# Fewer gathers in the gate phase, fewer U steps beside the drain, and the first splits of v one step earlier

## The chip, the cores and the metric

One core of one Trainium2 chip runs the whole program. The metric is device time in microseconds: the kernel before takes 1535.39 us (median of 3 runs, 1534.54 to 1535.76). The profiled execution, from which every duration below is read, took 1524.62 us, of which 1522.8 us lie between its first and its last instruction.

## The reference, cut to what matters

A decoder layer on 512 tokens of width 1024, in float32: a token mixer (gated linear attention beside a state-space group), and then PEER, a retrieval of single-neuron experts. The change lies in PEER alone:

```
q = (xt @ w_query)                      # 8 heads x 2 halves, 128 keys each
s = einsum('thpd,hpkd->thpk', q, sub_keys)
top_s, top_i = top_k(s, 16)             # per half; then the best 16 of the 16x16 sums
gate = softmax(best_s)
act = einsum('td,ted->te', x_blk, u[i_blk])
hid = gelu(act) * g_blk
out = einsum('te,ted->td', hid, v[i_blk])
```

There are 16384 experts (128 x 128 keys), u and v hold a row of 1024 for each, and each token uses 128 of them.

## The kernel before, in words

**Two ways to the experts.** The first 384 tokens (TD) don't gather. For them the kernel computes the activations of all 16384 experts, in 128 steps of 128 experts: U step e computes u·x for its 128 experts and 384 tokens, 24 matmuls in 8 parts of 3 (`u_part`, `rhs_part`, L857), because float32 is kept by splitting each operand into a high and a low part (`split`, L103 and L104: ScalarE copies the high part `uh`, L91, and VectorE, or GpSimd in some stages, subtracts to get the low part `ul`). V step e adds hid·v for the same 128 experts, 18 matmuls (6 groups of 3). The last 128 tokens gather their rows of u and v by an indirect DMA (`gather`, L1134), 128 gathers of u and 128 of v of 512 KB each; VectorE uses each in one instruction of 128x1024 (`use`, L100). Two gathers stay pending, so the use of one is written when the second after it is issued. There are three buffers (`gat`).

**The stages.** (1) The mixers. (2) The queries and scores, with 6 U steps in between. (3) The route: VectorE works out which experts each token has (`select`, four times two halves, `spread`), while TensorE is given 17 U steps, so that 23 are done. ScalarE's pieces of `ties(t)` (tile `k`), which wait for an earlier `select` to give up the buffer, are written between parts of the U steps. The low parts are made on GpSimd here. (4) The gate phase: 48 units of 8 tokens. For each unit VectorE builds one-hot tiles (A, eq, B), TensorE multiplies them (`pg`, L1185, 16 matmuls), ScalarE copies the gates of the later experts into `stage`, and VectorE multiplies the gates into `ring` for the U steps that are done. Between the units stand 32 U steps (steps 23 to 54), whose low parts VectorE makes, and 12 gathers, one after every fourth unit. Every 8 units the stage tile (128 partitions x 69 x 64, in two buffers) is written to device memory (`gd`), on ScalarE's DMA queue, in pieces of 256 bytes. (5) The drain: after the last unit the last stage tile is written out while U steps 55 to 58 run. (6) The V loop: V step e beside U step e+59 (as long as there is one), with the remaining gathers spread over it; `gload` reads the gates of step e+59 back from `gd` into the ring (59 steps long). The kernel's own constants are RING = 59 and LEFT, the number of U steps beside the drain.

**What sets the order.** Each engine runs its instructions in the order in which the program writes them. All loads of u, v, `gd` and the weights are issued by one queue (SyncE's, "SPq" in the profile), in order too: a load that has to wait holds all loads behind it. A U step's rows of u are loaded two steps ahead, and split one step ahead. Gathers are issued by GpSimd.

**Memory at the border of stages 4 and 6.** The gate phase's pool `gp` (A, eq, B, two stage tiles) is closed after the last unit, and the pool `vp` of the V loop (high and low parts `vh`, `vl` of v, raw blocks `vr`, the split gates `hh`, `hl`) takes the same place. `reuse_waits="tile"` makes each new tile wait only for the old tiles whose bytes it takes. In both pools the names lie one after the other in the order in which they are first asked for, each with all its buffers. In `gp` that is A (2 x 2048 bytes of a partition), eq (2048), B (2 x 4096) and stage (2 x 17664). In the kernel before the order in `vp` is vh (3 x 2048), vl (3 x 2048), vr (4 x 4096), hh (2 x 1536), hl (2 x 1536). Of the buffers of one name the first request takes the lowest, the second the highest, the next ones follow downwards.

Of the kernel before, what the change touches and what calls it, by code (L numbers as in the profile page):

```python
# [8 lines left out]
F32R = mybir.dt.float32r  # L9
# [16 lines left out]
TD = GT * 128  # L26
# [37 lines left out]
class Layer:  # L64
# [791 lines left out]
    def experts(self):  # L856
# [103 lines left out]
        def ties(t):  # L960
            x = (kp if t % 2 else self.kr).tile([128, 2, 8, 16, 16], F16, name="k8", tag="k8", bufs=1)
            for e in range(2):
                for g in (slice(0, 4), slice(4, 8)):
                    pieces.append((t, x[:, e, g], bc(tif[:, t, g, e, :], 3, 16)))
            TIE[t] = x
# [8 lines left out]
        def select(t):  # L974

            while any(p[0] == t for p in pieces):
                piece()
            ii = kp.tile([128, 2, 8, 16], F32, name="ii", bufs=2)
            for e in range(2):
                oh = c.tile([128, 8, 16, 16], F16, name="gat", tag="gat", bufs=3)  # L980
                tt(oh, bc(CF[0][:, e, t], 2, 16), bc(itj if e else its, 1, 8), OP.is_equal if e else OP.is_ge)
                tt(oh, oh, TIE[t][:, e], OP.mult)
                for n in (8, 4, 2):
                    tt(oh[:, :, 0:n, :], oh[:, :, 0:n, :], oh[:, :, n:2 * n, :], OP.add)
                tt(ii[:, e], oh[:, :, 0, :], oh[:, :, 1, :], OP.add)
            IX[t] = ii
# [9 lines left out]
        def gates2():  # L996
            sm = kp.tile([128, 2, NT, 8], F32, name="sm")
            V.tensor_reduce(sm[:, 0], bs, axis=AX.X, op=OP.add)
            V.reciprocal(sm[:, 1], sm[:, 0])
            tt(bs, bs, bc(sm[:, 1], 3, 16), OP.mult)  # L1000
# [10 lines left out]
        def spread(t):  # L1011
            ii, g = IX.pop(t), bs[:, t]
            p = pt()
            T.transpose(p[:, 0:128], flat(ii[:, 0]), ident)
            T.transpose(p[:, 128:256], flat(ii[:, 1]), ident)
            T.transpose(p[:, 256:384], flat(g), ident)
            act(gs[:, 0, t * 128:(t + 1) * 128], p[:, 256:384], AF.Copy, scale=SC)
            SPR[t] = p

        def spread2(t):  # L1020
            p = SPR.pop(t)
            s = slice(t * 128, (t + 1) * 128)
            V.tensor_copy(i2s[:, s], p[:, 128:256])
            V.tensor_copy(i1s[:, s], p[:, 0:128])
            stt(gs[:, 1, s], p[:, 256:384], SC, gs[:, 0, s], OP.mult, OP.subtract)
# [22 lines left out]
        def u_part(i, pool=False):  # L1048
            e = nu[0]
            if e >= NE:  # L1050
                return
            if i == 0:
                up[0] = pt()
            self.rhs_part(up[0][:, :TD], tsd, not hold[0] and nu[0] < RS - 4)
            if i in PP and pieces:
                piece()
            if i == 7:
                keep(e, up[0])
                nu[0] += 1

        def u_run(n):
            for _ in range(n):
                for i in range(8):
                    u_part(i)
# [23 lines left out]
        gates1()  # L1088
        select(0)
        gates2()  # L1090
        u_run(1)
        ties(2)
        u_run(1)
        select(1)
        u_run(1)
        spread(0)
        u_run(1)
        ties(3)
# [6 lines left out]
        select(3)  # L1105
        u_run(2)
        spread(2)
        u_run(3)
        spread2(2)
        idx = c.tile([128, 128], I32, name="idx")  # L1110
        gt0 = c.tile([128, 128], F32, name="gt0")
# [15 lines left out]
        def gather():  # L1127
            j = ng[0]
            if j < 256:
                ng[0] += 1  # L1130
                src = a["u"] if j < 128 else a["v"]
                r = c.tile([128, D], F32, name="gat", tag="gat", bufs=3)
                k = j % 128
                G.indirect_dma_start(out=r, out_offset=None, in_=src,  # L1134
                                     in_offset=bass.IndirectOffsetOnAxis(ap=idx[:, k:k + 1], axis=0))
                pend.append((j, r))
            if len(pend) > (2 if j < 256 else 0):
                use(*pend.pop(0))
# [22 lines left out]
        def gprep(u):  # L1161

            if u >= NU:
                return
            w = slice(u * UT, u * UT + UT)
            two = lambda x: bc(x.rearrange("p (a t) -> p a t", t=2), 2, 128)
            A = gp.tile([128, UT // 2, 128, 2], F16, name="A", bufs=2)
            eq = gp.tile([128, UT // 2, 128, 2], F16, name="eq")
            B = gp.tile([128, 2, UT // 2, 128, 2], F16, name="B", bufs=2)
            tt(A, bc(itx, 1, UT // 2), two(i2s[:, w]), OP.is_equal)  # L1170
            tt(eq, bc(itx, 1, UT // 2), two(i1s[:, w]), OP.is_equal)
            for i in range(2):
                tt(B[:, i], eq, two(gs[:, i, w]), OP.mult)
            AB[u] = A, B

        def gunit(u):

            A, B = AB.pop(u)
            if u % UPT == 0:
                stage[0] = gp.tile([128, NE - RS, ST], F32, name="stage", bufs=2)  # L1180
            p = self.ps.tile([128, UT * 128], F32, name="pg", bufs=2)
            for t in range(UT):
                o = p[:, t * 128:(t + 1) * 128]
                for i in range(2):
                    T.matmul(o, A[:, t // 2, :, t % 2], B[:, i, t // 2, :, t % 2], start=i == 0, stop=i == 1)  # L1185
            n = nu[0]
            p3 = p.rearrange("p (t k) -> p k t", t=UT)
            w = slice(u * UT, u * UT + UT)
            if n < RS:
                act(ring[:, n:, w], p3[:, n:RS, :], AF.Copy)  # L1190
            act(stage[0][:, :, u % UPT * UT:(u % UPT + 1) * UT], p3[:, RS:, :], AF.Copy)
            gprep(u + 1)
            release()
            tt(ring[:, :n, w], p3[:, :n, :], ring[:, :n, w], OP.mult)
            gtok[0] = w.stop
            if u % UPT == UPT - 1:
                t0 = u // UPT * ST
                self.S.dma_start(gd3[:, :, t0:t0 + ST], stage[0])


        HT = {}

        def hprep(e):
            if e >= NE:
                return
            HT[e] = [vp.tile([128, TD], F32R, name=n, bufs=2) for n in ("hh", "hl")]
            self.split(*HT[e], ring[:, e % RS, :])

        self.psum("psg")
        self.nbank = 4  # L1210
        hold[0] = True
        gprep(0)
        LEFT = 4
        parts = 8 * (RS - LEFT - nu[0])
        done = 0
        for u in range(NU):
            gunit(u)
            while done * NU < parts * (u + 1):
                u_part(done % 8)
                done += 1  # L1220
            if u % 4 == 3:
                gather()
        hold[0] = False
        release()
        gctx.close()
        vp = ctx.enter_context(tc.tile_pool(name="vp", bufs=1, reuse_waits="tile"))
        vs = Stream(self, vp, "v", [a["v"][e * 128:(e + 1) * 128, :] for e in range(NE)], 4)
        u_run(LEFT - 1)
        vs.loads(1)
        u_run(1)  # L1230
        vs.loads(3)
        vs.split(1)
        hprep(0)

        g0 = ng[0]
        share = [0]
# [79 lines left out]
        for e in range(NE):  # L1316
# [9 lines left out]
            if e == NE - 2:  # L1326

                hprep(e + 1)
                vs.split(2 * e + 2)
                vs.pair = us.pair  # L1330
                vs.split(2 * e + 3)
                final()
                break
            hh, hl = HT.pop(e)
# [6 lines left out]
            for i in range(3):  # L1341
                vgrp(0, i)
                if i == 2:
                    vs.parts.pop(2 * e)
                    vs.split(2 * e + 2)
                    hprep(e + 1)
                    gload(e + 1 + RS)
                u_part(i)
                fill(i)
# [113 lines left out]
```

## Time and profile before

| | us |
|---|---|
| median of 3 runs | 1535.39 |
| profiled execution | 1524.62 |
| its span | 1522.8 |
| TensorE busy in the span | 1473.2 (97%) |
| VectorE busy | 1166.3 (77%) |
| mean granted clock of TensorE | 0.992 |

PE is TensorE, DVE VectorE, ACT ScalarE, POOL GpSimd, SPq the queue of loads. Times are from the start of the span. Matmuls are pipelined: their records overlap, so a matmul's time is read from one start to the next.

| stage | us from the start |
|---|---|
| route, up to the first unit | 386 to 473.6 |
| gate phase, first unit to issue of the last stage write | 473.6 to 673.76 |
| drain, until V step 0 and U step 59 run without a break | 673.76 to 700 |
| V loop with U steps, V loop alone, final norm | 700 to 1522.8 |

### The profile page before, as it was taken

Reading aid. Unit: us, or ns where it says so; the run is one execution under the profiler, and the core shown is the slowest. Engines: PE = TensorE matmul, PEld = TensorE weight load, DVE = VectorE, ACT = ScalarE, POOL = GpSimd, SP = SyncE. Lnnn points to the kernel's source line nnn. Section 1 sums busy time; section 2 is a strip of 40 time slices with the busy share of each in tenths; the row PEclk is TensorE's granted clock in tenths of the full one; section 3 lists DMA queues with packets and bytes.
Section 4 is the critical chain, followed back from the end, with each engine's and each line's share of the span. In section 5 each row is a group of like instructions: output and inputs, shape, how many; then the busy total and the mean of one; then the engine's idle time right before and its main releaser. Section 6 shows DMA issues by size and latency. Waiting matters only on the chain.

```text
span 1522.8 us, 22405 instructions
## 1 busy us (share of the span) xinstructions
PE 1473.2 (97%) x7904; PEld 1284.2 (84%) x7904; DVE 1166.3 (77%) x2476; ACT 632.5 (42%) x1200; POOL 449.4 (30%) x378
## 2 busy tenths in 40 slices
PE   7999999999988999899999999999999999999997
PEld 5777767888988988787999999999999998888886
DVE  6543654599999999986777777787788877888886
ACT  5335623433653544443333333333333333434434
POOL 1002402444563000001333333333333333333332
PEclk9999999999999999999999999999999999999999
DMA  5231213322334556668889888888898987888894
GB/s 186 83 125 56 71 46 133 111 84 86 108 110 140 157 173 194 171 194 298 306 299 318 309 317 308 314 311 314 293 334 310 323 296 264 298 293 292 290 320 178
DMA packets 148738, 335.56 MB, mean 220 GB/s; under 512 B 64640, under 2 KB 73872, under 8 KB 148496
## 3 DMA queue, kind: packets, MB, share of 16 engines
q1 hardware_dynamic: 58672, 186.32, 36.1%
q0 software_dynamic: 36864, 134.23, 24.8%
q10 hardware_dynamic: 53088, 13.57, 3.9%
q8 instruction: 62, 1.02, 0.3%
q14 instruction: 52, 0.43, 0.1%
HBM read 315.79 MB, written 18.28 MB: 219 GB/s over the span
## 4 chain that ended last, share of the span: by engine, by line
PE 77%; DVE 14%; DMA 3%; issue 3%; ACT 2%; POOL 0%; SPq 0%; DVEq 0%; ACTq 0%; POOLq 0%
PE pm L109 24%; PE pm L110 24%; PE pm L108 24%; DVE gat L97 3%; DVE ul L104 2%; DMA gd<-stage 1%; DVE B L97 1%; PE pg L1185 1%; DVE eq L97 1%; DVE A L97 1%; DVE ring L97 1%; DMA ur<-in_uT 1%; PE pm L902 1%; DVE gat L100 1%; ACT b L91 1%
## 5 line engine op out<-in xcount | busy, mean ns | idle before, releaser
L108 PE MATMUL pm<-nT,uh 128*128 128x384 f32 (+1 forms) x1152 | 401.9, 349 | 3.5 <-ACT uh L91 3.0
L110 PE MATMUL pm<-nT,ul 128*128 128x384 f32 (+1 forms) x1152 | 396.9, 345 | 2.4 <-POOL ul L104 2.3
L109 PE MATMUL pm<-nT,uh 128*128 128x384 f32 (+1 forms) x1152 | 396.7, 344 | 0.5 <-DVE nT L97 0.5
L110 PE MATMUL pm<-vh,hl 128*128 128x512 f32 x765 | 300.7, 393 | 1.2 <-DVE hl L104 1.2
L108 PE MATMUL pm<-vh,hh 128*128 128x512 f32 x765 | 298.9, 391 | 2.3 <-ACT hh L91 2.0
L109 PE MATMUL pm<-vl,hh 128*128 128x512 f32 x765 | 300.4, 393 | 0.2 <-DVE vl L104 0.2
L1134 POOL DMA_INDIRECT gat<-in_u,idx x128 | 137.1, 1071 | 471.1 <-DVE gat L100 461.3
L91 ACT ACTIVATE uh<-ur 128x512 fp32r<-128x512 f32 x288 | 180.4, 629 | 211.7 <-PE pm L109 190.1
L108 PEld LDWEIGHTS pm<-nT,uh 128*128 128x128 f32 x1152 | 217.8, 189 | 28.3 <-ACT uh L91 3.6
L109 PEld LDWEIGHTS pm<-nT,uh 128*128 128x128 f32 x1152 | 217.7, 189 | 25.1 <-DVE nT L97 1.1
L110 PEld LDWEIGHTS pm<-nT,ul 128*128 128x128 f32 x1152 | 217.6, 189 | 9.9 <-POOL ul L104 3.4
L1134 POOL DMA_INDIRECT gat<-in_v,idx x128 | 146.8, 1147 | 267.0 <-DVE n2a L100 229.5
L91 ACT ACTIVATE vh<-vr 128x512 fp32r<-128x512 f32 x255 | 159.4, 626 | 136.8 <-PE pm L110 135.4
L104 DVE TENSOR_TENSOR vl<-vr,vh 128x512 fp32r<-128x512 f32 x255 | 175.1, 688 | 41.9 <-ACT vh L91 41.5
L104 DVE TENSOR_TENSOR ul<-ur,uh 128x512 fp32r<-128x512 f32 x208 | 142.0, 689 | 58.2 <-ACT uh L91 57.9
L100 DVE SCALAR_TENSOR_TENSOR n2a<-gat,dots,n2a 128x1024 f32<-128x1024 f32 x128 | 163.8, 1280 | 11.8 <-DMA gat<-in_v,idx 8.3
L110 PEld LDWEIGHTS pm<-vh,hl 128*128 128x128 f32 x765 | 144.0, 188 | 32.4 <-DVE hl L104 1.6
L108 PEld LDWEIGHTS pm<-vh,hh 128*128 128x128 f32 x765 | 143.9, 188 | 16.7 <-ACT hh L91 2.3
L100 DVE SCALAR_TENSOR_TENSOR gat<-gat,n2a 128x1024 f32<-128x1024 f32 x128 | 156.0, 1218 | 1.7 <-DMA gat<-in_u,idx 1.6
L109 PEld LDWEIGHTS pm<-vl,hh 128*128 128x128 f32 x765 | 143.9, 188 | 13.9 <-DVE vl L104 0.5
L104 POOL TENSOR_TENSOR ul<-ur,uh 128x512 fp32r<-128x512 f32 x80 | 116.2, 1460 | 98.4 <-ACT uh L91 98.2
L91 ACT ACTIVATE gl<-pm 128x384 f32<-128x384 f32 (+16 forms) x105 | 46.5, 443 | 222.7 <-PE pm L110 136.8
(254 smaller groups left out, 1707.6 us busy)
## 6 DMA issues: line engine op xcount, KB each, us to landing
ur<-in_uT SPq DMA_DIRECT2D x128, 512.0 KB
vr<-in_v SPq DMA_DIRECT2D x128, 512.0 KB
gd<-stage ACTq DMA_DIRECT2D x6, 2208.0 KB
ring<-gd SPq DMA_DIRECT2D x69, 192.0 KB
wraw<-in_w_in SPq DMA_DIRECT2D x23, 512.0 KB
ur<-in_w_query SPq DMA_DIRECT2D x16, 512.0 KB
b<-in_x SPq DMA_DIRECT2D x8, 512.0 KB
wraw<-in_w_out SPq DMA_DIRECT2D x8, 512.0 KB
```

The costliest lines, as they stand in the source:

```text
L91: return self.S.activation(out, in_, f, **k)
L97: return self.V.tensor_tensor(out, x, y, op=op)
L100: return self.V.scalar_tensor_tensor(out, x, s, y, op0=op0, op1=op1, **k)
L104: (self.G if pool else self.V).tensor_tensor(lo, src, hi.bitcast(F32), op=OP.subtract)
L108: T.matmul(out, lhi, rhi, start=start, stop=False)
L109: T.matmul(out, lhi, rlo, start=False, stop=False)
L110: T.matmul(out, llo, rhi, start=False, stop=stop)
L902: T.matmul(p[:, t * 128:(t + 1) * 128], q[:, t * 128:(t + 1) * 128], skT[:, b, :], start=True, stop=True)
L1134: G.indirect_dma_start(out=r, out_offset=None, in_=src, in_offset=bass.IndirectOffsetOnAxis(ap=idx[:, k:k + 1], axis=0))
L1185: T.matmul(o, A[:, t // 2, :, t % 2], B[:, i, t // 2, :, t % 2], start=i == 0, stop=i == 1)
```

## The change

There are four edits. In the route one U step moves from behind `select(1)` to ahead of `ties(2)`, and one more is added at the end (18 in place of 17). In the gate phase a gather follows every twelfth unit in place of every fourth (4 calls in place of 12); the other 8 calls are spread over the V loop by the same plan. LEFT goes from 4 to 2: the gate phase has 33 U steps (24 to 56) and the drain two (57 and 58). Around these two the order of the drain is new: the first `hh`, `hl` are asked for ahead of the first v blocks, loads of v blocks 0 and 1 stand ahead of both U steps, the splits of v block 0 and of the first gates between them, loads of v blocks 2 and 3 behind them.

```diff
@@ route
         gates2()
-        u_run(1)
+        u_run(2)
         ties(2)
         u_run(1)
         select(1)
-        u_run(1)
         spread(0)
@@
         spread(2)
-        u_run(3)
+        u_run(4)
         spread2(2)
@@ gate phase and drain
+        def htile():
+            return [vp.tile([128, TD], F32R, name=n, bufs=2) for n in ("hh", "hl")]
+
         def hprep(e):
             if e >= NE:
                 return
-            HT[e] = [vp.tile([128, TD], F32R, name=n, bufs=2) for n in ("hh", "hl")]
+            if e:
+                HT[e] = htile()
             self.split(*HT[e], ring[:, e % RS, :])
...
-        LEFT = 4
+        LEFT = 2
         parts = 8 * (RS - LEFT - nu[0])
...
-            if u % 4 == 3:
+            if u % 12 == 11:
                 gather()
...
         vs = Stream(self, vp, "v", [a["v"][e * 128:(e + 1) * 128, :] for e in range(NE)], 4)
-        u_run(LEFT - 1)
+        HT[0] = htile()
         vs.loads(1)
         u_run(1)
-        vs.loads(3)
         vs.split(1)
         hprep(0)
+        u_run(1)
+        vs.loads(3)
```

## Rows read from the trace of the kernel before

**Rows 1.** The page, busy time and share of the span of each engine:
```profile
PE 1473.2 (97%) x7904; PEld 1284.2 (84%) x7904; DVE 1166.3 (77%) x2476; ACT 632.5 (42%) x1200; POOL 449.4 (30%) x378
```
**Rows 2.** Busy time by stretch: start:end length, engines (instructions), clock, DMA share, GB/s:
```profile
473.60:480.00 6.40, 6.00 (x34) 5.84 (x34) 4.36 (x8) 2.08 (x4) 1.80 (x2) 0.63 0.74 246
472.40:673.80 201.40, 187.00 (x1527) 174.35 (x1528) 194.56 (x351) 91.93 (x221) 12.98 (x12) 0.99 0.58 169
673.80:693.40 19.60, 19.00 (x107) 18.04 (x105) 9.72 (x16) 7.23 (x14) 1.01 (x1) 1.00 0.97 302
693.40:706.60 13.20, 10.03 (x43) 8.69 (x44) 7.63 (x13) 4.52 (x9) 1.93 (x2) 0.87 0.75 250
706.60:715.00 8.40, 8.40 (x44) 7.61 (x43) 7.00 (x12) 3.10 (x6) 2.44 (x3) 1.00 0.73 246
800.00:1100.00 300.00, 300.00 (x1516) 271.70 (x1515) 232.84 (x396) 112.08 (x218) 96.45 (x91) 1.00 0.89 310
```
**Rows 3.** What TensorE waited for in the gate phase: us, times, longest:
```profile
PE pg L1185 <- DVE B L97: 13.0, 31, 1.3
```
**Rows 4.** Groups of VectorE's instructions in the gate phase: busy us, mean ns | idle before:
```profile
L104 DVE TENSOR_TENSOR ul<-ur,uh 128x512 fp32r<-128x512 f32 x63 | 41.9, 684 | 4.6 <-ACT uh L91 4.4
...
L97 DVE TENSOR_TENSOR ring<-pg,ring 128x184 f32<-128x184 f32 (+31 forms) x48 | 22.6, 471 | 0.5 <-ACT stage L91 0.5
L100 DVE SCALAR_TENSOR_TENSOR gat<-gat,n2a 128x1024 f32<-128x1024 f32 x9 | 11.0, 1219 | 0.0
L97 DVE TENSOR_TENSOR ring<-gl,ring 128x16 f32<-128x16 f32 (+30 forms) x31 | 11.0, 353 | 0.0
```
**Rows 5.** The chain of waits through the drain: start, us, what:
```profile
673.76 22.84 DMA gd<-stage
696.69 0.57 DVE hl L104
```
**Rows 6.** TensorE in order of time, around the drain (start, us, what, idle before):
```profile
680.14 0.34 PE L108 MATMUL pm<-nT,uh 128*128 128x384 f32 x1
...
684.30 0.34 PE L108 MATMUL pm<-nT,uh 128*128 128x384 f32 x1
...
695.37 0.50 PE L108 MATMUL pm<-vh,hh 128*128 128x512 f32 x1 [2.03 <-ACT hh L91]
...
697.30 0.79 PE L110 MATMUL pm<-vh,hl 128*128 128x512 f32 x1 [1.20 <-DVE hl L104]
697.89 0.52 PE L108 MATMUL pm<-nT,uh 128*128 128x384 f32 x1
```
**Rows 7.** ScalarE in order of time, in the route:
```profile
405.86 0.63 ACT L91 ACTIVATE uh<-ur 128x512 fp32r<-128x512 f32 x1 [1.04 <-DMA ur<-in_uT]
...
420.88 1.05 ACT L91 ACTIVATE k<-tif 128x1024 f16<-128x1024 f16 x1 [4.40 <-DVE gat L97]
```
**Rows 8.** TensorE at the start of the gate phase:
```profile
473.64 0.29 PE L1185 MATMUL pg<-B,A 128*128 128x128 f16 x1 [5.49 <-DVE B L97]
```
**Rows 9.** VectorE in the route, the same three additions twice:
```profile
420.88 1.47 DVE L97 TENSOR_TENSOR gat<-gat 128x1024 f16<-128x1024 f16 x3
...
435.00 3.42 DVE L97 TENSOR_TENSOR gat<-gat 128x1024 f16<-128x1024 f16 x3
```
**Rows 10.** The queue of loads in order of time, route and drain:
```profile
401.58 0.33 SPq L88 DMA_DIRECT2D ur<-in_uT  x1
...
675.76 0.33 SPq L88 DMA_DIRECT2D ur<-in_uT  x1
...
690.20 0.43 SPq L88 DMA_DIRECT2D vr<-in_v  x1
...
696.61 0.33 SPq L88 DMA_DIRECT2D vr<-in_v  x1
```
**Rows 11.** DMA rate in 40 slices, 672 to 702 us, then 636 to 656 us:
```profile
GB/s 55 0 0 9 221 218 217 218 217 139 144 331 384 286 411 389 438 336 293 294 353 416 405 424 400 395 332 426 401 422 84 23 2 0 224 386 348 163 228 311
...
GB/s 0 0 0 0 0 131 164 295 243 298 301 283 285 280 272 253 237 226 220 135 133 152 359 417 366 263 335 441 382 297 286 292 344 217 360 346 123 25 8 0
```

## The prediction

> **What bounds the kernel now.** The busy table comes first: TensorE works 97% of the span [rows 1], so what can still be won is its idle 50 us. The table by stretch says where these lie [rows 2]. From 800 to 1100 us TensorE is busy in every microsecond, with VectorE at 78% and the DMA engines at 0.89: the V loop is TensorE's. From 472.4 to 673.8 it is another engine's: VectorE is busy 194.6 of 201.4 us, TensorE 187.0, and TensorE's only wait there is for VectorE's tile B, 13.0 us in 31 pieces [rows 3]. The reader is to see two facts together: VectorE full, and TensorE waiting for it alone. There the uses of gathers (9 of 1219 ns) lie on the engine that bounds, while in the V loop VectorE has room for them [rows 2, 4].
>
> The third place is the drain. The chain of waits runs through one transfer: the last stage tile, issued at 673.76, takes 22.84 us, and the low part hl waits for it [rows 5]. TensorE first waits 2.03 us for hh, then 1.20 us for hl, and then its matmuls follow at 0.32 us in place of 0.17 [rows 6]: in the stretch 693.4 to 706.6 its granted clock is 0.87 on average, so part of it was at the lower level, 1.2 GHz [rows 2]. The fourth is the route: ScalarE stands 4.40 us in front of a tie piece at 420.88 that VectorE holds up, with the high parts of the next U step behind it [rows 7], and at the gate phase's start TensorE has waited 5.49 us for B [rows 8].
>
> **Gate phase: what goes and what comes.** Twelve calls leave ten uses before the V loop, four leave two. The use of the last unit stands behind the last gate product in both kernels (before: nine in the window), so eight leave the part that VectorE bounds. From one start to the next a use takes 1.15 us: 8 x 1.15 = 9.2 us less. One U step more costs VectorE two low parts (684 ns each, 0.60 from start to start: 1.2 us), one product of gelu and gate (353 ns, 0.3 net) and one more row of 8 tokens in each of 48 gate products (471 ns for 39 rows on average, so some 8 ns each: 0.4 us) [rows 4]. Net: 9.2 - 1.9 = 7.3 us off the gate phase. TensorE pays 24 matmuls for the new step, 684.30 - 680.14 = 4.16 us [rows 6]. It has 201.4 - 187.0 = 14.4 us idle, and 191.2 us of work fit into the 194.1 us that remain [rows 2], so VectorE still bounds, by 3 us. If the engines, going step by step, cannot use these 3 us, the gate phase gives 4 in place of 7.3; more than 9.2 it cannot give.
>
> **Route.** U step 23 is new there, 4.16 us of TensorE. The step moved ahead of `ties(2)` runs where ScalarE stands before [rows 7]; TensorE then reaches the transposes that wait for `select(2)` some 4 to 5 us earlier and waits there, and behind them has four U steps (16.6 us) where three and an idle 5.49 us stood [rows 8]. 3 x 4.16 + 5.49 = 18.0 us hold them and about one microsecond of a clock that has to rise again. The cover is thin, and its price if gone is small: at 473.6 to 480 the clock is 0.63 on average before, which costs 6.4 x 0.37 = 2.4 us [rows 2], and that stretch would now start warmer. What is not covered is GpSimd beside VectorE. The same three additions take VectorE 1.47 us when GpSimd makes no low part and 3.42 us when it does [rows 9]. The new step brings two low parts on GpSimd: 0 if they fall where VectorE doesn't mind, 1.95 us for one such group. The moved step costs the quiet at 420.88 and gives it back at 450, where GpSimd runs dry. I take +0.5 us, with bounds -2 (the slow start gone) and +2.6.
>
> By the Trainium skill ("SBUF — State Buffer", section "Who interferes with whom") a VectorE instruction with two SBUF inputs and a GpSimd instruction that reads SBUF lock each other out for a whole instruction. The rows agree, 1.47 against 3.42 us [rows 9]. By the rule alone each of the two new low parts could hold VectorE for its full length, and the term would be its upper bound; I keep +0.5 because the row also shows places where GpSimd has nothing to do.
>
> **The drain: removed.** Call T the issue of the last stage write (673.76 before). Before, TensorE ends U step 60 beside V step 1 at 715.0 [rows 2], T + 41.2. Without two U steps that would be T + 32.9. The waits for hh and hl (3.2 us) go, since the splits now stand ahead of the last U step and hh, hl move in memory.
>
> **The drain: what is late next.** This is the term that decides. With hh and hl asked for first, vr moves up. In bytes from the start of the pool: the gate phase's second stage tile lies at 32000 to 49664 and is the one being written out (six tiles, the last in the second buffer). Before, hl starts at 31744 and overlaps it, which is the wait in the chain [rows 5]. After, vh and vl end at 12288, hh and hl at 18432, and vr is 18432 to 34816. v block 0 takes the lowest buffer, v block 1 the highest, 30720 to 34816: it overlaps the stage tile by 2816 bytes. So the load of v block 1 has to wait for the drain, and it stands on the queue of loads ahead of everything else: ur of steps 59 and 60, v blocks 2 and 3, the first `gload`. That a load can stand so is to be seen before, where the fourth v block is issued only at 696.61, 6 us after the third [rows 10].
>
> How long does it stand? The stage tile alone moves at 218 GB/s [rows 11]: 2208 KB, 10.4 us. It starts 1.4 us after T, and before, eight loads of 512 KB run beside it (those issued from 675.76 to 690.20, seven on the queue [rows 10], and one gather): (22.84 - 1.4 - 10.4) / 8 = 1.38 us each. The drain that began at 638.25 carries four loads and by this sum takes 10.4 + 5.5 = 15.9 us; the row shows 16 [rows 11]. After, two remain (v block 0 and one gather): T + 1.4 + 10.4 + 2.8 = T + 14.6. Then v block 1 and ur of step 59 are issued, 0.5 us apart; a load on a quiet queue takes 405.86 - 401.58 = 4.3 us until ScalarE starts on it [rows 7, 10], the one ahead adds 0.9: T + 20.3. The high part adds 0.6: T + 20.9. TensorE has ended U steps 57 and 58 and the first group of V step 0 at T + 1.6 + 8.3 + 0.7 = T + 10.6. It stands 10.3 us.
>
> What is left is 15.95 us (two V steps beside two U steps, 8.32 each, less the first group), and the clock at the lower level after the wait, 2.4 us as at 473.6 [rows 2]: T + 39.3. Against T + 41.2 the drain gives 2 us: 8.3 us of steps moved out, 6.4 us of new idle. Bounds: nothing waits, T + 27, gives 14; a drain as long as before (22.84 us) puts the load 8.2 us later, T + 47.5, and costs 6.
>
> **V loop.** 252 gathers in place of 244: 0.09 more in each of 69 steps of 8.3 us, and fewer behind. TensorE is never idle there, the DMA engines stand at 0.89 and would go to 0.90, VectorE from 0.78 to 0.79 [rows 2]. I cost it at nothing; TensorE's work is the cover. If it were gone, eight transfers of 1.38 us are 11 us.
>
> **Sum.** -7.3 + 0.5 - 2 = -8.8 us; the profiled execution goes from 1524.62 to 1515.8. It lies 10.8 us under the median of the runs, which I take as the same for both: 1535.4 - 8.8 = 1526.6 us.
>
> **Rivals.** *A, the forecast:* -8.8, 1526.6.
>
> *B, v block 1 does not hold the queue* (another place in memory, or a drain that is over in time). For it: the edit takes hl off the stage tile. Against it: the sum of bytes above. The loads then all run beside the drain, seven of them: it ends at T + 1.4 + 10.4 + 9.7 = T + 21.5; `gload` and ur of step 61 come behind, the latter 5.2 us later, and U step 61 starts at T + 28 to 31 where A has 39.3. The drain gives 10 instead of 2: 1519.
>
> *C, TensorE takes over the gate phase.* For it: 191.2 of 194.1 us, by turns with VectorE. Against it: TensorE waits for B alone now [rows 3], and those waits shrink with VectorE's load. 4 in place of 7.3, and a drain a little longer (no gain): -3.5, 1532.
>
> *D, slower: the V loop's transfers become the bound.* For it: DMA engines at 0.89 on average leave little for a gather that comes late, and VectorE, in order, then holds the splits. Against it: not one idle microsecond of TensorE in 300 [rows 2]. It decides from the point where the buffers ahead run empty; the price is 8 x 1.38 = 11.0 us and one fall of the clock, 2.4: -8.8 + 13.4 = +4.6, 1540.
>
> **How the numbers follow.** A 0.52, B 0.16, C 0.20, D 0.12. What a measurement of this kernel can tell from no change is 0.2%, 3.1 us. Faster: nearly all of A (0.49), B, some less than half of C: 0.73. Within: the rest of C, a bit of A and D: 0.18. Slower: most of D, 0.09. The range leaves out the outer half of B and of D: 1518 to 1537.
>
> **What would show it.** Gate phase: from the first `pg` to the last stage write 194 us instead of 200, VectorE still full, one use of a gather in it. Drain: SPq stands in front of the second v block until the stage write ends, some 14.6 us after its issue; ScalarE waits for ur, TensorE some 10 us, then matmuls at 0.32 us apart. Route: no 4.40 us in front of the tie piece, the first unit within a microsecond of 473.6. V loop: TensorE busy throughout. Wrong if SPq does not wait there (then B), if TensorE's waits for B in the gate phase stay at 13 us (then its length does too), or if TensorE is idle in the V loop (D).

## The result and the profile after

Against the kernel before, run beside it, the changed kernel takes 1524.9 us (median of 17 runs) where the kernel before takes 1534.34: ratio 0.9935, 95% interval 0.9917 to 0.9953, which is 10.0 us of 1534.3 (7.2 to 12.7). The forecast was -8.8 us and 1526.6 us.

The profiled execution tells something else at first sight: it took 1525.01 us, its span is 1523.2 us, and the one before took 1524.62 us with a span of 1522.8. So the stages first.

Busy time by stretch, after (columns as in [rows 2]): the gate phase from the first `pg` to the last stage write, the drain up to and from the stop, and 300 us of the V loop.

```profile
475.20:668.90 193.70, 188.38 (x1551) 178.09 (x1552) 186.46 (x336) 93.21 (x225) 2.93 (x3) 0.99 0.55 160
668.90:679.50 10.60, 10.60 (x62) 10.39 (x60) 6.49 (x11) 4.22 (x8) 1.01 (x1) 1.00 0.77 204
679.50:698.00 18.50, 10.38 (x43) 8.95 (x42) 7.11 (x12) 4.47 (x9) 2.09 (x2) 0.82 0.90 305
800.00:1100.00 300.00, 300.00 (x1495) 270.47 (x1494) 233.57 (x399) 110.88 (x216) 100.09 (x93) 1.00 0.89 311
```

The gate phase is 193.7 us instead of 200.1 (473.64 to 673.76 before), with one U step more in it. VectorE is nearly as full as before, 186.5 of 193.7 us against 194.6 of 201.4 [rows 2], but TensorE's busy time is now the larger of the two, 188.4 us. What TensorE waited for there, after, and the uses of gathers that are left on VectorE:

```profile
PE pg L1184 <- DVE B L97: 8.3, 17, 3.3
```
```profile
L100 DVE SCALAR_TENSOR_TENSOR gat<-gat,n2a 128x1024 f32<-128x1024 f32 x1 | 1.2, 1221 | 0.0
```

The longest of the 17 waits, 3.3 us, is the one that ends with the first `pg`. Inside the gate phase 5.0 us in 16 pieces are left, where [rows 3] has 13.0 in 31.

The drain, in three views. The chain of waits through it (start, us, what):

```profile
668.88 13.30 DMA gd<-stage
682.67 4.46 DMA ur<-in_uT
...
687.21 0.64 ACT uh L91
687.89 0.69 PE pm L108
```

The queue of loads, and TensorE:

```profile
682.25 0.33 SPq L88 DMA_DIRECT2D vr<-in_v  x1
682.67 0.86 SPq L88 DMA_DIRECT2D ur<-in_uT  x2
683.58 1.07 SPq L88 DMA_DIRECT2D vr<-in_v  x2
684.69 0.44 SPq L88 DMA_DIRECT2D ring<-gd  x1
```
```profile
687.89 0.69 PE L108 MATMUL pm<-nT,uh 128*128 128x384 f32 x1 [8.12 <-ACT uh L91]
```

The reader is to see one load, v block 1 at 682.25, 13.4 us after the stage write's issue at 668.88, and the five loads behind it, all issued within 2.5 us. TensorE stands 8.12 us for the high part of U step 59. The stage write itself is over in 13.3 us in place of 22.84 [rows 5], because the loads that ran beside it before now stand on the queue; with more loads beside it, in e3 and e7 below, it takes 15.2 and some 17.8 us.

U step 60 is done (ScalarE starts its gelu `gl`) at 706.22, before at 715.10:

```profile
706.22 0.49 ACT L91 ACTIVATE gl<-pm 128x384 f32<-128x384 f32 x1 [3.24 <-PE pm L110]
```
```profile
715.10 0.49 ACT L91 ACTIVATE gl<-pm 128x384 f32<-128x384 f32 x1 [3.18 <-PE pm L110]
```

That is 8.9 us ahead. These 8.9 us are lost again between 706 and 1278 in this pair of executions, and the table by stretch shows how: in the 300 us from 800 to 1100 TensorE is busy throughout in both, but runs 1495 matmuls where the execution before ran 1516 [rows 2]. This pace is no effect of the change. The same kernels, profiled once more (labels before_again and after_again below), show the kernel before at 1494:

```profile
800.00:1100.00 300.00, 300.00 (x1494) 270.41 (x1493) 229.57 (x392) 110.41 (x215) 96.12 (x90) 1.00 0.86 306
```

All twelve profiles of this document have 1494 or 1495 matmuls there, or 1516 or 1517: an execution has one of two paces in that stretch. The profile before caught the quicker one, and with it 1524.62 us where most of its runs take 1531 to 1536.

### The profile page after: what moved, and what is told of

It is laid out like the page before. It is cut to its first block, busy times and chain, and to the rows that moved or that the text cites. A ratio compares the mean times of both kernels' runs of the same rounds, so it can differ in the third digit from the quotient of the medians.

```text
span 1523.2 us, 22401 instructions
## 1 busy us (share of the span) xinstructions
PE 1479.2 (97%) x7904; PEld 1290.1 (85%) x7904; DVE 1168.4 (77%) x2473; ACT 632.3 (42%) x1201; POOL 451.6 (30%) x380
## 4 chain that ended last, share of the span: by engine, by line
PE 53%; issue 20%; DVE 13%; POOL 9%; DMA 3%; ACT 2%; POOLq 0%; SPq 0%; DVEq 0%; ACTq 0%
PE pm L108 16%; PE pm L109 16%; PE pm L110 16%; POOL gat L1133 8%; DVE gat L97 4%; PE pg L1184 2%; DVE ul L104 1%; DVE B L97 1%; PE pm L902 1%; DMA gd<-stage 1%; DVE ring L97 1%; DVE eq L97 1%; DVE A L97 1%; ACT b L91 1%; DMA gat<-in_u,idx 1%
```

## Experiments

Here, too, T is the issue of the last stage write, and "done" is the start of a step's `gl`. Each kernel was timed beside the kernel before, but for the last pair, which was run once each.

**One part alone: the gathers.** Kernel before, with:

```diff
-            if u % 4 == 3:
+            if u % 12 == 11:
                 gather()
```

> The kernel before with one edit: a gather after every twelfth unit, not every fourth (4 calls in the gate phase, 248+4 spread later). Theory (VectorE bounds the gate phase, the V loop hides gathers): eight uses of 1.15 us leave, so the gate phase, from the first pg matmul to the issue of the last stage write, goes from 200.1 to about 191 us, and TensorE ends U step 60 about 9 us earlier; time -9 us, ratio 0.994. Rival C (TensorE takes over): 196 us or more, -4 us at most. Rival D (transfers bound the V loop): gate phase as the theory has it, but TensorE idle in the V loop and the time within 3 us of before.

Measured: 1521.25 against 1533.09 us, ratio 0.9937 (0.9916 to 0.9959): all of the change's gain. The gate phase runs from the first `pg` at 473.9 to a stage write at 663.85, 189.9 us:

```profile
663.85 0.52 ACTq L1198 DMA_DIRECT2D gd<-stage  x1
```

200.1 - 189.9 = 10.2 us, where eight uses of 1.15 us are 9.2. Rival C is out in this kernel, whose gate phase has the 32 U steps of before. Rival D is out as a cause of loss, but not wholly: TensorE waits once in the V loop, 0.5 us (1.0 in the changed kernel, below).

**The same from the other side.** Changed kernel, with that edit undone (`u % 4 == 3`):

> The changed kernel with its one gather edit undone (a gather after every fourth unit, 12 in the gate phase). Theory (the gain is the gathers'): 8 uses of 1.15 us come back, the gate phase from first pg matmul to last stage write goes from 193.7 to about 202.5 us; drain as in the changed kernel, U step 60 at T + 37 to 38; time within 2 us of before, ratio 0.999. Rival (the drain or the route brings a good part): ratio 0.996 or lower.

Measured: 1532.35 against 1533.26 us, ratio 1.0013 (0.999 to 1.0037). From the first `pg` (473.4) to the stage write (675.7) it is 202.3 us, U step 60 is done at T + 37.0. Route, drain and LEFT together bring nothing that these runs can tell.

That is not because each of them does nothing. The profile of e1 and that of the changed kernel ran at the same pace (1495 matmuls in 300 us) and can be laid side by side. In the changed kernel the first `pg` comes at 475.2 instead of 473.9, the gate phase takes 193.7 us instead of 189.9, and U step 60 is done at T + 37.3 instead of T + 42.8: +1.3, +3.7 and -5.4 us. The drain is shorter because it has two U steps less, and the route and the gate phase, which have one of them each, pay for it. LEFT alone was not tried.

**One part alone: the route.** Kernel before with the two edits of the route, LEFT left at 4:

```diff
-        u_run(1)
+        u_run(2)
         ties(2)
...
-        u_run(1)
         spread(0)
...
-        u_run(3)
+        u_run(4)
         spread2(2)
```

> The kernel before with the route's edits alone (18 U steps in the route, one of them moved ahead of the ties; LEFT stays 4, so the gate phase has 31 U steps). Theory: the first pg matmul comes 1 to 2 us later (GpSimd's two more low parts slow VectorE), the gate phase is 1.9 us shorter for one U step less: 0 us in all, ratio 1.000. Rival (the moved step removes a stall of 4.4 us that counts): first pg no later than before, time -3 to -5 us. Rival (the gate phase's length is TensorE's): it is 4.2 us shorter, one U step, time -2 to -3 us.

Measured: 1526.69 against 1533.09 us, ratio 0.9988 (0.9962 to 1.0013), no difference to be told. First `pg` at 475.5, gate phase 199.4 us. One U step less shortens the gate phase by 0.7 to 1.5 us (before: 200.1, and 200.9 when profiled again), not by TensorE's 4.2, so VectorE is what counts there, with 12 gathers in it.

**One part alone: the drain's order.** Kernel before with the new order around the last two of its four U steps:

```diff
-        u_run(LEFT - 1)
+        u_run(LEFT - 2)
+        HT[0] = htile()
         vs.loads(1)
         u_run(1)
-        vs.loads(3)
         vs.split(1)
         hprep(0)
+        u_run(1)
+        vs.loads(3)
```

> The kernel before with the new order of the drain alone (hh and hl asked for first, v blocks 0 and 1 loaded ahead of the last two U steps, splits of v block 0 between them); LEFT stays 4 and the gate phase keeps its 12 gathers. Theory (v block 1 waits for the stage write and holds ur of step 59, but four U steps now cover most of the wait): the stage write takes some 15 us in place of 22.8, TensorE stops about 2 us ahead of U step 59, U step 60 ends at T + 37 to 38 in place of T + 41.3; route and gate phase as before: -4 us, ratio 0.9975. Rival (the held queue costs more than the waits for hh and hl did): T + 42 or later, ratio 1.000 or above.

Measured: 1533.43 against 1533.61 us, ratio 1.0003 (0.9981 to 1.0025). My -4 us is a miss, and the rival came true. U step 60 is done at T + 42.6, not 37 to 38: v block 1 goes out at 692.81, T + 17.8, where I had put 15, though four loads run beside the write and the prediction's own sum gives T + 17.3. Behind it ur of step 59 comes so late that TensorE waits 2.98 us, and then runs at the lower level of its clock (granted 0.50 from 698.35 to 702 us, which is 1.2 GHz):

```profile
692.81 0.33 SPq L88 DMA_DIRECT2D vr<-in_v  x1
693.23 0.86 SPq L88 DMA_DIRECT2D ur<-in_uT  x2
```
```profile
698.35 0.69 PE L108 MATMUL pm<-nT,uh 128*128 128x384 f32 x1 [2.98 <-ACT uh L91]
```

The kernel before, at the same pace (before_again), has U step 60 done at T + 42.7. The old waits for hh and hl cost the same as the new one.

**Does v block 1 hold the queue?** Changed kernel, v block 1 loaded behind ur of steps 59 and 60:

```diff
         HT[0] = htile()
-        vs.loads(1)
+        vs.loads(0)
```

> The changed kernel with one load moved: of v blocks 0 and 1 only block 0 is loaded ahead of the last two U steps, block 1 after them, so it no longer stands ahead of the loads of U steps 59 and 60. Theory (the load of block 1 waits for the stage write and holds the queue): TensorE runs through V step 0 and stops only ahead of V step 1, some 4 to 5 us in place of 8.1; U step 60 ends about T + 33 (T = issue of the last stage write) where the changed kernel has T + 37.3: -4 us against the changed kernel, ratio to before 0.991. Rival (the drain's transfers as such are slow, whatever stands ahead): ur of step 59 lands no earlier, T + 37, no gain.

Measured: 1516.48 us, ratio to before 0.9907 (0.9876 to 0.9937), some 8 us under the changed kernel in place of 4. U step 60 is done at T + 28.9 instead of T + 37.3. v block 1 still waits for the stage write (issued at 686.16, T + 15.2), but of what TensorE needs next only v block 1's own splits depend on it, and TensorE stops for 1.46 us:

```profile
690.94 0.50 PE L108 MATMUL pm<-vh,hh 128*128 128x512 f32 x1 [1.46 <-ACT hh L91]
```

I had put the stop at 4 to 5 us; the load landed 3.7 us after its issue and left less. The rival (the drain as such is slow) is out.

**Without the overlap.** Changed kernel with three raw buffers of v, so that `vr` ends at byte 30720, below the stage tile:

```diff
-... for e in range(NE)], 4)
+... for e in range(NE)], 3)
-            vs.loads(e + 4)
+            vs.loads(e + 3)
```

(and `bufs=3` where the last step takes a `vr` tile)

> The changed kernel with three raw buffers of v in place of four (loads one step less ahead), so that no tile of the V loop lies on the stage tile that is being written. Theory: no load of v waits for the drain; TensorE runs through to the end of U step 60 at T + 27 to 28, and waits some 3 us ahead of V step 2, because the first gload and ur of step 61 stand behind the drain, which takes about 21 us with seven loads beside it. -6 to -7 us against the changed kernel, ratio to before 0.989. Rival 1 (the drain bounds whatever the order): U step 60 ends at T + 35 or later, no gain. Rival 2 (three buffers starve the V loop): the gain at U step 60 is there, and TensorE is idle later in the V loop.

Measured: 1515.78 us, ratio 0.9885 (0.9849 to 0.9922). U step 60 at T + 26.9. Then, as expected, the first `gload` holds ur of step 61: ScalarE waits 5.36 us, TensorE half a microsecond (I had put 3), and U step 61 is done at T + 36.3:

```profile
693.74 0.63 ACT L91 ACTIVATE uh<-ur 128x512 fp32r<-128x512 f32 x1 [5.36 <-DMA ur<-in_uT]
...
705.64 0.49 ACT L91 ACTIVATE gl<-pm 128x384 f32<-128x384 f32 x1 [3.24 <-PE pm L110]
```

Three buffers don't starve the V loop: TensorE waits for nothing from 720 to 1480 us.

**The last wait taken out.** The kernel with three raw buffers, and the first `gload` behind the first part of U step 59:

```diff
-        gload(RS)
...
                 u_part(i)
+                if e == 0 and i == 0:
+                    gload(RS)
                 fill(i)
```

> The kernel with three raw buffers of v, and the first gload moved behind the first part of U step 59, so that the load of ur of step 61 stands ahead of it on the queue and does not wait for the drain. Theory (what is left after the drain is the queue's order): in the kernel with three raw buffers U step 60 ends at T + 26.9 and U step 61 at T + 36.3, one microsecond late; here U step 61 ends at T + 35.2 to 35.5, -1 us, ratio to before 0.988. Rival (VectorE's product of step 59, which waits for the first gload, then comes later and holds the splits): U step 61 at T + 37 or later.

Measured: 1508.21 against 1533.26 us, ratio 0.9864 (0.9833 to 0.9894). TensorE doesn't wait at all; U steps 59, 60 and 61 follow at 8.32 us, U step 61 done at 704.72, T + 35.2:

```profile
688.08 0.49 ACT L91 ACTIVATE gl<-pm 128x384 f32<-128x384 f32 x1 [3.18 <-PE pm L110]
696.40 0.49 ACT L91 ACTIVATE gl<-pm 128x384 f32<-128x384 f32 x1 [3.18 <-PE pm L110]
704.72 0.49 ACT L91 ACTIVATE gl<-pm 128x384 f32<-128x384 f32 x1 [3.18 <-PE pm L110]
```

The median is 7.6 us under that of the version before, but the wait is only 1 us of it: the two profiles differ in pace, too (1494 matmuls in 300 us there, 1517 here).

**No use of a gather in the gate phase.** The same with one call, behind the last unit:

```diff
-            if u % 12 == 11:
+            if u == 47:
```

> The best version so far (three raw buffers, first gload behind the first part of U step 59) with one gather call in the gate phase in place of four, behind the last unit, so that no use of a gather lies in the gate phase. Theory (VectorE still bounds there, TensorE has some 2 us of room): one use less, the gate phase 192.5 us in place of 193.7, time -1 us, which the runs cannot tell from none; the V loop takes 255 gathers without idle. Rival (TensorE bounds by now): the gate phase stays at 193.5 or more.

Measured: 1505.59 against 1533.61 us, ratio 0.9836 (0.9807 to 0.9864), the lowest of all. The gate phase is 192.6 us, as forecast; the five other profiles with four gathers and 33 U steps there (the changed kernel twice, e3, e4, e5) have 193.4 to 194.7. So one use less still shortens it, and VectorE counts, but TensorE is the busier engine, 188.1 us against 185.3. Of the 7.5 us that it waits for B, 3.3 us lie ahead of the first `pg`:

```profile
476.20:668.80 192.60, 188.09 (x1550) 177.98 (x1551) 185.28 (x333) 93.23 (x225) 1.74 (x2) 0.99 0.55 159
```
```profile
PE pg L1184 <- DVE B L97: 7.5, 15, 3.3
```

**The two paces.** Both kernels once more:

> The kernel before once more, for the pace of the V loop. Theory (an execution has one of two paces while U and V steps run side by side, 8.32 or 8.44 us a step, which is 8 us in 69 steps and does not depend on the kernel): a time of 1531 us or more goes with some 500 matmuls in 100 us, one of 1526 or less with 506 or 507. Rival (the slower pace belongs to kernels with 252 gathers in the V loop): 506 or 507 here, whatever the time.

> The changed kernel once more, for the same question. Theory of two paces: a time of 1518 us or less goes with 506 or 507 matmuls in 100 us, one of 1523 or more with 500. Rival (the pace belongs to the number of gathers): 500 here, whatever the time.

Measured: the kernel before 1536.09 us with 1494 matmuls in 300 us, the changed kernel 1525.13 us with 1494. The first fits the theory of two paces and puts the rival out, since a kernel with 244 gathers has the slower pace too; the second fits both. The quicker pace with many gathers is seen in the two best versions, 1505.91 and 1505.22 us in their profiled executions, here the last one:

```profile
800.00:1100.00 300.00, 300.00 (x1516) 271.81 (x1515) 238.45 (x405) 112.61 (x219) 101.97 (x96) 1.00 0.89 319
```

Two executions at the same, slower pace can be compared: 1536.09 and 1525.13 us, 11.0 apart, of which 9.9 are there when U step 60 is done (718.51 and 708.65 us): +3.0 in the route, -7.4 in the gate phase, -5.4 in the drain.

## Why the prediction was right, and where it was not

**Gate phase: the sum right, two of its terms not.** 194 us were forecast, 193.7 measured. The whole phase gave 6.4 us, and 7.4 in the second pair of profiles, where 7.3 were forecast. But eight uses alone took 10.2 us off (forecast 9.2, e1), and the U step that was added cost 3.7 us (e1 beside the changed kernel), where the sum had 1.9. These two misses offset each other, and that is luck. The step behind the second one is "VectorE still bounds, by 3 us": it holds TensorE's 191.2 us of work against the 194.1 us of time that remain, and not against VectorE's work, which by the same sum falls to some 187 us (194.6 - 7.3). Measured, TensorE is busy 188.4 us and VectorE 186.5. With 12 gathers a U step is worth 0.7 to 1.5 us of the phase (e2), as long as VectorE has the more to do; with four it costs nearly the 4.16 us that TensorE takes for it. So a part of rival C came true. How the engines' turns make up the rest was not separated.

**Route: undersized.** The first `pg` comes at 475.2 (477.9 when profiled again), not within a microsecond of 473.6 (474.9 when profiled again). Starts scatter: in the eight profiles with the new route they lie between 473.4 and 477.9 us (475.66 on average), in the four with the old one between 473.6 and 474.9 (474.35). That is some 1.3 us, between the +0.5 that I took and the upper bound of 2.6. One piece of it is the same in every profile: the group of three additions that took 2.43 us (at 467.89) behind the last U step's low parts before takes 4.41 us now beside two more on GpSimd:

```profile
467.51 4.41 DVE L97 TENSOR_TENSOR gat<-gat 128x1024 f16<-128x1024 f16 x3
```

That is 2.0 us, the difference that [rows 9] shows. The quiet that I expected GpSimd to give back at 450 did not come; the same group at 450.09 takes 4.37 us. The Trainium skill's rule of the lock ("SBUF — State Buffer", section "Who interferes with whom") speaks for the upper bound. In this group the trace agrees with it, 4.41 us against 2.43. The moved step did not remove the stall in front of the tie piece, either: it still takes 2.70 us, at 422.37 (before 4.40 us, [rows 7]):

```profile
422.37 1.06 ACT L91 ACTIVATE k<-tif 128x1024 f16<-128x1024 f16 x1 [2.70 <-DVE gat L97]
```

**Drain: the mechanism right, its size not.** v block 1 waits for the stage write at the head of the queue. The queue stands from v block 0 to v block 1 (two loads in one row of 17.64 us):

```profile
664.94 17.64 SPq L88 DMA_DIRECT2D vr<-in_v  x2
```

Forecast was an issue at T + 14.6, measured T + 13.4. The sum had two loads beside the write, v block 0 and a gather. v block 0 went out 3.9 us ahead of T and, by the 4.3 us of a load on a quiet queue, was over before the write began at T + 1.4; with the gather alone the sum gives T + 13.2. Then ur of step 59 took 4.46 us, where the sum has 5.2. TensorE's stop: forecast 10.3 us, measured 8.1; U step 60 at T + 37.3 instead of T + 39.3. Against the kernel before, T + 41.3 and T + 42.7 in its two profiles, the drain gives 4.0 to 5.4 us, not 2. Shown by undoing: with v block 1 off the head (e3) or off the stage tile (e4) the stop is 1.5 us or none. So the new order, meant or not, trades one wait for another and alone gives nothing measurable (e7), and what two U steps less give, the route and the gate phase pay (e6).

**V loop: hidden, but for one microsecond.** TensorE waits 0.98 us once, at 1104, where the gathers pass from u to v: VectorE stands 4.50 us for the residual rows (`n2a<-hd`), and the low part of v behind it:

```profile
1102.14 1.28 DVE L100 SCALAR_TENSOR_TENSOR n2a<-gat,dots,n2a 128x1024 f32<-128x1024 f32 x1 [4.50 <-DMA n2a<-hd]
```

All three profiles with 252 gathers in the V loop and a drain not repaired show such a wait (0.5 us in e1, 1.0 and 1.1 in the changed kernel). None with 244 gathers shows it, nor one with 252 or more and the drain repaired. So the number of gathers alone does not make it; which detail decides was not tried.

**The sum held by luck, too.** At the same pace (before_again and after_again) the terms are +3.0, -7.4 and -5.4 us, where +0.5, -7.3 and -2 were forecast: the misses of route and drain have opposite signs.

**The step that failed: the profile's own time.** I took the 10.8 us between profiled execution and median as the same for both kernels and said that the profiled time would go to 1515.8. It was 1525.01. The 10.8 us are no constant: some 8 of them are the quicker pace of one execution. The forecast of the median held all the same because it was formed as a difference of stages that the pace hardly touches.

## What to carry to other kernels

Before a tile is moved in memory to free it from a wait, list what moves into the bytes that it leaves, and what stands behind that on its queue: here the split that waited 1 us was freed, and the load that took its place held five others (the first of them went out at T + 13.8, and at T + 2.0 where nothing held it, e4). Loads that must wait belong behind those that need not. Work taken off a full engine is worth its time from start to start, as long as the second engine's busy time leaves room; to see that, compare the work of the one with the work of the other as both will be after the change, not with the time that remains.

## What the runs showed that was not expected

While U and V steps run side by side, one execution has either 8.32 us a step (506 matmuls in 100 us) or 8.44 (some 499), from the first step to the last, with TensorE busy throughout and its granted clock at 1.00, the level of 2.4 GHz, in both. Over 69 steps that is 8 us. Both kinds of matmul lose the same 3 ns: those of 384 columns follow at 0.173 or 0.176 us, those of 512 at 0.232 or 0.235. With V steps alone there is one pace, 442 or 443 matmuls in 100 us, in all profiles, and U steps alone take 4.16 us in all. The pace itself is seen in profiles alone; by their times the kernel before had the slower one in most runs, and the two best versions the quicker one in nearly all of theirs, which adds to their ratio: at the quicker pace the kernel before takes 1524.62 us and the best version 1505.22, 19 us less, while the medians are 28 us apart. What sets the pace stays open.
